# RMS normalisation with relu, 16384 rows of 512 floats: an unrolled program rewritten as hardware loops, with the arithmetic of a row regrouped

## The chip, the cores and the metric

One core of one Trainium2 chip. The metric is the device time of one execution in microseconds (us). The kernel before takes 164.29 us (median of 4 runs, 164.16 to 164.57). The profile is one traced execution, and its "span" (162.0 us) leaves out some 2 us of start and end that the time includes.

## The reference

```python
# x: 16 x 1024 x 512 float32; gamma: 512 ones; eps: 1e-5
rms = np.sqrt(np.mean(x ** 2, axis=-1, keepdims=True) + eps)
return np.maximum(x / rms * gamma, 0).astype(np.float32)
```

33.55 MB come in and 33.55 MB go out, and little arithmetic is done on them.

## The kernel before

The rows are cut into 8 chunks of 4 MB (128 partitions x 16 rows x 512). There are six slots in on-chip memory, so six loads can go out before any store, and a seventh waits until the first store has landed. All loads and stores are issued from SP, on one queue. A chunk is worked on in two groups of 8 rows.

```python
K = 16; G = 8; nslots = 6
junk = psum.tile([P, d], F32, name="junk")
...
def compute(i):
    xt = slot[i % nslots]
    for g in range(ngroups):                       # 2 groups of 8 rows
        a, b = g * G, (g + 1) * G
        for j in range(a, b):                      # ScalarE: sum of squares of a row
            nc.scalar.activation(out=junk, in_=xt[:, j, :], func=ACTF.Square,
                                 accum_out=ss[i][:, j:j + 1])
        nc.scalar.activation(out=rms[i][:, a:b], in_=ss[i][:, a:b],
                             func=ACTF.Sqrt, bias=eps_sb, scale=inv_d)
        nc.vector.tensor_mul(out=xt[:, a:b, :], in0=xt[:, a:b, :], in1=gammaG())
        nc.vector.reciprocal(out=rstd[i][:, a:b], in_=rms[i][:, a:b])
        for j in range(a, b):                      # VectorE: scale and relu of a row
            nc.vector.tensor_scalar(out=xt[:, j, :], in0=xt[:, j, :],
                scalar1=rstd[i][:, j:j + 1], scalar2=0.0, op0=ALU.mult, op1=ALU.max)
...
for i in range(min(nslots, nchunks)): load(i)
for i in range(min(nslots, nchunks)): compute(i)
nxt = nslots
for i in range(nchunks):
    store(i)
    if i >= 1 and nxt < nchunks:
        load(nxt); compute(nxt); nxt += 1
```

Everything is unrolled, and the framework places the semaphore waits. A wait that it places is carried by the waiting instruction itself.

Of the kernel before, what the change touches and what calls it, by code (L numbers as in the profile page):

```python
# [1 line left out]

# [4 lines left out]

F32 = mybir.dt.float32
ALU = mybir.AluOpType
ACTF = mybir.ActivationFunctionType  # L10


@with_exitstack
def kernel(
    ctx: ExitStack,
    tc: tile.TileContext,
    x: bass.AP,
    gamma: bass.AP,
    eps: bass.AP,
    out: bass.AP,  # L20
):


    nc = tc.nc
    P = nc.NUM_PARTITIONS

    x2 = x.flatten_outer_dims()
    out2 = out.flatten_outer_dims()
    n, d = x2.shape
    rows = n // P  # L30
    inv_d = 1.0 / d
    xv = x2.rearrange("(c p k) d -> c p k d", p=P, k=16)
    ov = out2.rearrange("(c p k) d -> c p k d", p=P, k=16)

    K = 16
    G = 8
    nchunks = rows // K
    nslots = 6
    ngroups = K // G

    singles = ctx.enter_context(tc.tile_pool(name="singles", bufs=1))
    slots = ctx.enter_context(tc.tile_pool(name="slots", bufs=1))
    small = ctx.enter_context(tc.tile_pool(name="small", bufs=1))
    psum = ctx.enter_context(
        tc.tile_pool(name="psum", bufs=1, space=bass.MemoryType.PSUM))

    ctx.enter_context(tc.manual_schedule())

    gseed = singles.tile([P, d], F32, name="gseed")
    gamma_sb = singles.tile([P, d], F32, name="gamma_sb")  # L50
    eps_sb = singles.tile([P, 1], F32, name="eps_sb")
    junk = psum.tile([P, d], F32, name="junk")
    slot = [slots.tile([P, K, d], F32, name=f"slot{s}") for s in range(nslots)]
    ss = [small.tile([P, K], F32, name=f"ss{i}") for i in range(nchunks)]
    rms = [small.tile([P, K], F32, name=f"rms{i}") for i in range(nchunks)]
    rstd = [small.tile([P, K], F32, name=f"rstd{i}") for i in range(nchunks)]

    def load(i):
        nc.sync.dma_start(out=slot[i % nslots], in_=xv[i])

    def store(i):
        nc.sync.dma_start(out=ov[i], in_=slot[i % nslots])

    def gammaG():
        g = gamma_sb[:]
        return bass.AP(tensor=g.tensor, offset=g.offset,
                       ap=[g.ap[0], [0, G], g.ap[1]])

    def compute(i):
        xt = slot[i % nslots]  # L70
        for g in range(ngroups):
            a, b = g * G, (g + 1) * G
            for j in range(a, b):
                nc.scalar.activation(out=junk, in_=xt[:, j, :], func=ACTF.Square,  # L74
                                     accum_out=ss[i][:, j:j + 1])
            nc.scalar.activation(out=rms[i][:, a:b], in_=ss[i][:, a:b],  # L76
                                 func=ACTF.Sqrt, bias=eps_sb, scale=inv_d)
            nc.vector.tensor_mul(out=xt[:, a:b, :], in0=xt[:, a:b, :], in1=gammaG())  # L78
            nc.vector.reciprocal(out=rstd[i][:, a:b], in_=rms[i][:, a:b])  # L79
            for j in range(a, b):  # L80
                nc.vector.tensor_scalar(  # L81
                    out=xt[:, j, :], in0=xt[:, j, :],
                    scalar1=rstd[i][:, j:j + 1], scalar2=0.0,
                    op0=ALU.mult, op1=ALU.max)

    nc.vector.memset(gseed, 0.0)  # L86
    nc.vector.memset(eps_sb, eps)  # L87
    for q in range(0, P, 32):
        nc.scalar.dma_start(out=gseed[q:q + 1, :], in_=gamma[None, :])

    for i in range(min(nslots, nchunks)):
        load(i)
    nc.vector.stream_shuffle(gamma_sb, gseed, [0] * 32)  # L93
    for i in range(min(nslots, nchunks)):
        compute(i)
    nxt = nslots
    for i in range(nchunks):
        store(i)
        if i >= 1 and nxt < nchunks:
            load(nxt)  # L100
            compute(nxt)
            nxt += 1


# [1 line left out]
_INS = ['x', 'gamma', 'eps']  # L106
_OUTS = [((16, 1024, 512), 'float32')]

_NUMBERS = {'eps': 9.999999747378752e-06}


# [26 lines left out]
```

## Time and profile before

| | before |
|---|---|
| time, median (lowest to highest) | 164.29 us (164.16 to 164.57) |
| span of the profile | 162.0 us |
| share of the 16 DMA engines' time on the data queue | 96.9% |
| VectorE (DVE) at work, first multiply to last row | 19.1 to 143.0 us |
| last store, issue to landing | 143.0 to 161.0 us |

The page of the kernel before. After the busy times come rows over 40 equal slices of the span: for DMA the mean busy share in tenths, then GB/s. The queue lines give packets, MB and share of the engines' time. In the group lines the numbers after the bar are busy us and mean ns of one, then idle time before them and what ended it.

```profile
span 162.0 us, 554 instructions
...
DVE 124.6 (77%) x164; ACT 98.5 (61%) x274; POOL 0.2 (0%) x4
...
DMA  6999899999999999998999999999999999999990
GB/s 227 421 405 502 388 413 493 390 421 477 396 421 471 396 388 388 461 445 388 463 437 404 453 445 404 453 437 396 461 429 445 429 421 445 429 421 445 437 413 16
...
q1 hardware_dynamic: 2304, 67.11, 96.9%
q14 instruction: 3, 0.02, 0.0%
...
DVE 74%; DMA 8%; ACT 3%; issue 2%; DVEq 0%
...
L74 ACT ACTIVATE junk<-slot 128x512 f32<-128x512 f32 x128 | 76.8, 600 | 23.0 <-DMA slot<-in_x_dram 19.5
L78 DVE TENSOR_TENSOR slot<-slot,gamma_sb 128x4096 f32<-128x4096 f32 x16 | 70.7, 4418 | 4.2 <-ACT junk L74 4.2
L81 DVE TENSOR_SCALAR slot<-slot,rstd 128x512 f32<-128x512 f32 x128 | 52.1, 481 | 0.6
```

The DMA row is full from end to end. The chain (the line that begins "DVE 74%") names VectorE all the same: VectorE is seamless too, and a chain can follow only one of two things that run side by side.

The timeline of the kernel before: start, duration, engine, operation, and in brackets the idle time before it. First lines: ScalarE's (ACT) first rows. Then a group on VectorE, and the end.

```profile
13.06 0.60 ACT L74 ACTIVATE junk<-slot 128x512 f32<-128x512 f32 x1 [8.57 <-DMA slot<-in_x_dram]
13.60 0.19 ACT L74 ACTIVATION_READ_ACCUMULATOR junk<-slot 128x1 f32 x1
13.81 0.60 ACT L74 ACTIVATE junk<-slot 128x512 f32<-128x512 f32 x1
...
19.09 4.42 DVE L78 TENSOR_TENSOR slot<-slot,gamma_sb 128x4096 f32<-128x4096 f32 x1 [4.16 <-ACT junk L74]
23.43 0.20 DVE L79 RECIPROCAL rstd<-rms 128x8 f32<-128x8 f32 x1
23.66 3.26 DVE L81 TENSOR_SCALAR slot<-slot,rstd 128x512 f32<-128x512 f32 x8
26.83 4.42 DVE L78 TENSOR_TENSOR slot<-slot,gamma_sb 128x4096 f32<-128x4096 f32 x1
...
139.73 3.26 DVE L81 TENSOR_SCALAR slot<-slot,rstd 128x512 f32<-128x512 f32 x8
143.01 0.33 SPq L62 DMA_DIRECT2D out_dram<-slot  x1
```

VectorE's group has a period of 7.74 us (26.83 - 19.09).

The waits of the SP queue before: who waited for what, total us, times, longest.

```profile
SPq L133 <- DMA out_dram<-slot: 17.6, 1, 17.6
```

The last store needs 17.6 us after its issue is done.

### The profile page before, as it was taken

How to read it: one execution, taken by the hardware profiler on the slowest of the kernel's cores; microseconds unless marked ns; L12 is line 12 of the kernel's file. 1: busy time of each engine (PE TensorE's matmuls, PEld its weight loads, DVE VectorE, ACT ScalarE, POOL GpSimd, SP SyncE). 2: the span in 40 equal slices, each digit the busy share in tenths (PEclk: the TensorE clock that was granted, in tenths of full speed). 3: DMA queues.
4: the chain of work that ended last, by engine and by line, in shares of the span. 5: the costliest groups of instructions: out<-in, count | busy, mean ns of one | idle time of the engine just before them, and what ended most of it. 6: DMA issues, size and time to landing. Idle time of an engine off the chain costs nothing.

```text
span 162.0 us, 554 instructions
## 1 busy us (share of the span) xinstructions
DVE 124.6 (77%) x164; ACT 98.5 (61%) x274; POOL 0.2 (0%) x4
## 2 busy tenths in 40 slices
DVE  1001299999999999999999999999999999920000
ACT  2107999999999999999999199901998000000000
POOL 0000000000000000000000000000000000000000
DMA  6999899999999999998999999999999999999990
GB/s 227 421 405 502 388 413 493 390 421 477 396 421 471 396 388 388 461 445 388 463 437 404 453 445 404 453 437 396 461 429 445 429 421 445 429 421 445 437 413 16
DMA packets 2315, 67.14 MB, mean 414 GB/s; under 512 B 260, under 2 KB 260, under 8 KB 264
## 3 DMA queue, kind: packets, MB, share of 16 engines
q1 hardware_dynamic: 2304, 67.11, 96.9%
q14 instruction: 3, 0.02, 0.0%
q10 hardware_dynamic: 8, 0.01, 0.0%
HBM read 33.56 MB, written 33.55 MB: 414 GB/s over the span
## 4 chain that ended last, share of the span: by engine, by line
DVE 74%; DMA 8%; ACT 3%; issue 2%; DVEq 0%
DVE slot L78 43%; DVE slot L81 30%; DMA slot<-in_x_dram 8%; ACT junk L74 3%; DVE rstd L79 1%; DVEq L133 0%
## 5 line engine op out<-in xcount | busy, mean ns | idle before, releaser
L74 ACT ACTIVATE junk<-slot 128x512 f32<-128x512 f32 x128 | 76.8, 600 | 23.0 <-DMA slot<-in_x_dram 19.5
L78 DVE TENSOR_TENSOR slot<-slot,gamma_sb 128x4096 f32<-128x4096 f32 x16 | 70.7, 4418 | 4.2 <-ACT junk L74 4.2
L81 DVE TENSOR_SCALAR slot<-slot,rstd 128x512 f32<-128x512 f32 x128 | 52.1, 481 | 0.6
L74 ACT ACTIVATION_READ_ACCUMULATOR junk<-slot 128x1 f32 x128 | 23.8, 186 | 0.0
L93 DVE LOAD_MASK_SELECT gamma_sb<-gseed x1 | 0.0, 14 | 12.8 <-DMA gseed<-in_gamma_dram 12.8
L76 ACT ACTIVATE rms<-ss,eps_sb 128x8 f32<-128x8 f32 x16 | 4.8, 301 | 0.5
L74 ACT ACT_TABLE_LOAD x1 | 1.3, 1283 | 3.2 <-issue 3.2
L79 DVE RECIPROCAL rstd<-rms 128x8 f32<-128x8 f32 x16 | 3.1, 194 | 0.0
L76 ACT ACT_TABLE_LOAD x1 | 1.3, 1283 | 0.0
L86 DVE MEMSET gseed<- 128x512 f32 x1 | 0.5, 485 | 0.9 <-PEq L119 0.9
L93 DVE STREAM_SHUFFLE gamma_sb<-gseed 128x512 f32<-128x512 f32 x1 | 0.7, 721 | 0.0
L119 POOL MEMSET const-bfloat16-1.0<- 128x1 bf16 x1 | 0.1, 101 | 0.0
L119 POOL MEMSET const-uint8-127<- 128x1 uint8 x1 | 0.1, 101 | 0.0
L119 POOL MEMSET const-float32-0.0<- 128x1 f32 x1 | 0.1, 99 | 0.2 <-issue 0.2
L119 POOL MEMSET const-float32-1.0<- 128x1 f32 x1 | 0.1, 98 | 0.0
L87 DVE MEMSET eps_sb<- 128x1 f32 x1 | 0.1, 59 | 0.0
## 6 DMA issues: line engine op xcount, KB each, us to landing
slot<-in_x_dram SPq DMA_DIRECT2D x8, 4096.0 KB, 30.6
out_dram<-slot SPq DMA_DIRECT2D x8, 4096.0 KB, 35.4
gseed<-in_gamma_dram ACTq DMA_DIRECT2D x4, 2.0 KB
```

Of the source, the lines that this page charges most:

```text
L74: nc.scalar.activation(out=junk, in_=xt[:, j, :], func=ACTF.Square, accum_out=ss[i][:, j:j + 1])
L76: nc.scalar.activation(out=rms[i][:, a:b], in_=ss[i][:, a:b], func=ACTF.Sqrt, bias=eps_sb, scale=inv_d)
L78: nc.vector.tensor_mul(out=xt[:, a:b, :], in0=xt[:, a:b, :], in1=gammaG())
L79: nc.vector.reciprocal(out=rstd[i][:, a:b], in_=rms[i][:, a:b])
L81: nc.vector.tensor_scalar(out=xt[:, j, :], in0=xt[:, j, :], scalar1=rstd[i][:, j:j + 1], scalar2=0.0, op0=ALU.mult, op1=ALU.max)
L86: nc.vector.memset(gseed, 0.0)
L87: nc.vector.memset(eps_sb, eps)
L93: nc.vector.stream_shuffle(gamma_sb, gseed, [0] * 32)
L119: nc = _bacc.Bacc("TRN2", target_bir_lowering=False, num_devices=1)
```

## The change

Its intent: a shorter program and cheaper waits. The loops over groups become hardware loops on ScalarE and VectorE with semaphores of the kernel's own; one activation table is loaded ahead instead of two; the gamma multiply over 8 rows and the scale-and-relu per row become (x*rstd)*gamma per row and one relu over 8 rows.

```diff
+    junk = psum.tile([P, G, d], F32, name="junk")          # a scratch row for each of the 8
-        nc.sync.dma_start(out=slot[i % nslots], in_=xv[i])
+        nc.sync.dma_start(out=slot_ap(i), in_=xv[i]).then_inc(sem_ld[i], 16)
...
+        for i in range(nchunks):                            # GpSimd relays the landings
+            nc.gpsimd.wait_ge(sem_ld[i], 16)
+            nc.gpsimd.sem_inc(ready, per)
...
+        nc.scalar.preload_act_table(ACTF.Sqrt)
+        with nc.scalar.Fori(0, ngroups) as gi:
+            nc.scalar.wait_ge(ready, 1)
+            nc.scalar.sem_inc(ready, -1)
+            ...                                             # 8 squares, the last one: then_inc(sa, 1)
+            nc.scalar.wait_ge(sa, 1)
+            nc.scalar.sem_inc(sa, -1)
+            ...                                             # root: then_inc(sq, 1)
-            nc.vector.tensor_mul(out=xt[:, a:b, :], in0=xt[:, a:b, :], in1=gammaG())
-            nc.vector.reciprocal(out=rstd[i][:, a:b], in_=rms[i][:, a:b])
-            for j in range(a, b):
-                nc.vector.tensor_scalar(... op0=ALU.mult, op1=ALU.max)
+        with nc.vector.Fori(0, ngroups) as gi:
+            nc.vector.wait_ge(sq, 1)
+            nc.vector.sem_inc(sq, -1)
+            nc.vector.reciprocal(out=rstd[:, bass.ds(col, G)],
+                                 in_=rms[:, bass.ds(col, G)]).then_inc(sv, 1)
+            nc.vector.wait_ge(sv, 1)
+            nc.vector.sem_inc(sv, -1)
+            for j in range(G):
+                row = slots[:, bass.ds(base + j * d, d)]
+                r = nc.vector.scalar_tensor_tensor(
+                    out=row, in0=row, scalar=rstd[:, bass.ds(col + j, 1)], in1=gamma_sb,
+                    op0=ALU.mult, op1=ALU.mult)             # the last one: then_inc(sv, 1)
+            nc.vector.wait_ge(sv, 1)
+            nc.vector.sem_inc(sv, -1)
+            nc.vector.tensor_scalar_max(out=blk, in0=blk, scalar1=0.0).then_inc(done, 1)
```

The order of loads and stores on SP stays as it was.

## The prediction

> **What bounds the kernel now.** The transfers. Over the span of 162.0 us the SP queue's packets fill 96.9% of the 16 DMA engines' time (queue table); by stretches the DMA share is 0.97 to 1.05 from 5 to 155 us, at 420 to 453 GB/s. The Trainium skill ("DMA: Bandwidth & Descriptors", Bandwidth) gives 435 GB/s as the fabric's ceiling; the trace agrees. The chain of waits names VectorE (74%), because its work from 19.1 to 143.0 us is seamless and the last store follows it. But that store takes 17.6 us to land (waits of the SP queue), where the first load, at the head of the queue, needs 12.3 us. So the last store queues some 5.3 us behind others: VectorE has that much slack.
>
> **What changes, per group of 8 rows.** VectorE before, start to start (the chain): gamma multiply 4.33, reciprocal 0.12, eight row operations 0.41 apart (3.26): 7.74 us, 16 groups 123.9. After, the row operation reads two tensors. The Trainium skill ("VectorE: DVE Perf Modes", the perf-mode tier table) has fp32 one-source operations at double rate, two-tensor ones at single rate; the trace agrees: 4418 ns for 4096 elements against 481 for 512. Estimates from these: a row is 512 x 1.042 = 533 ns plus the 214 that the present row has over 267, so 747 ns long, 0.67 apart, eight rows 5.46; relu over 4096 elements at double rate 2.2; reciprocal 0.19. Together 7.85. Two waits on VectorE's own semaphore become instructions of their own, the first followed by a register instruction, where today reciprocal to row leaves 0.03 us. I guess 0.3 and 0.2 us for them; no record of before shows such a sequence. Sum 8.35 us, 0.6 more per group. Branch and address arithmetic should hide under the relu and the rows.
>
> **Head.** One table load (1.28 us) goes, but it lay beside VectorE's first multiply and gains nothing. VectorE now starts after the first root instead of beside it, and the landing is relayed through GpSimd: start about 20.1 instead of 19.1. ScalarE (0.76 us per row, about 6.9 per group) stays faster than VectorE, off the path.
>
> **Sum.** VectorE ends at 20.1 + 16 x 8.35 = 153.7 instead of 143.0, 10.7 later; slack absorbs 5.3; the end moves by some 5 us, less if the guessed waits are smaller (8.15 per group: about 2). The transfers are the same bytes in the same order. I predict 168.3 us, 80% range 165.0 to 172.5. Chances: faster by over 2% 0.01, within 2% 0.41, slower by over 2% 0.58.
>
> **What the profile would show.** Right: rows near 745 ns, 0.67 apart; relu near 2.28 us; VectorE's group period 8.15 to 8.6, its end at 150 to 157 us; the DMA share falling for 2 to 8 us before the last store; that store landing in about 12 us. Wrong: a period of 8.0 or less (the slack swallows all, the time stays near 164), or a last store that still queues.
>
> **What would make it wrong.** Own-semaphore waits nearly free; a row operation with less fixed cost than the present one; or, to the other side, a branch or register instructions that stall VectorE by a microsecond per group (+16 us), or ScalarE's loop becoming the slower one. The store alone may land in other than 12.3 us, which moves the end by as much.

## The result, and the profile after

| | before | after |
|---|---|---|
| time, median (lowest to highest), 4 runs each | 164.29 us (164.16 to 164.57) | 165.41 us (165.27 to 165.50) |
| ratio | | 1.0065 (95%: 1.0048 to 1.0083) |
| span | 162.0 us | 163.5 us |
| VectorE's first operation; period of a group; end | 19.09; 7.74; 142.99 us | 19.29; 8.24; 151.25 us |
| last landing, from the span's start | 160.97 us | 162.38 us |
| from VectorE's end to the last landing | 17.98 us | 11.13 us |

A ratio is the mean time of one kernel's fast runs over that of the other's of the same rounds, so it is not quite the ratio of the medians quoted. The change costs 0.65%: within 2%, but clear of noise.

The page after:

```profile
span 163.5 us, 1007 instructions
...
DVE 126.0 (77%) x164; ACT 86.3 (53%) x273; POOL 0.2 (0%) x4
...
DMA  6999999899999999989999999999999999993985
GB/s 232 409 394 498 393 433 465 385 473 425 401 489 393 425 345 417 481 385 441 457 401 473 409 409 441 433 433 433 417 433 457 417 433 433 441 433 160 385 385 257
...
q1 hardware_dynamic: 2304, 67.11, 96.3%
...
L108 ACT ACTIVATE junk<-slots 128x512 f32 x128 | 74.5, 582 | 30.5 <-ACTq L104 30.2
L132 DVE SCALAR_TENSOR_TENSOR slots<-slots,rstd,gamma_sb 128x512 f32 x128 | 86.2, 747 | 4.8 <-DVEq L129 4.8
L139 DVE TENSOR_SCALAR slots<-slots x16 | 36.7, 2294 | 2.4 <-DVEq L138 0.2
```

The DMA row now has a hole (the 3, slice 37, 147 to 151 us, 160 GB/s): the engines had run out of work when VectorE delivered the last chunk. The q14 line is gone. A row costs 747 ns, the relu 2294.

The timeline after, the same places:

```profile
13.55 0.60 ACT L108 ACTIVATE junk<-slots 128x512 f32 x1 [8.97 <-ACTq L104]
14.08 0.19 ACT L108 ACTIVATION_READ_ACCUMULATOR junk<-slots  x1
14.18 0.58 ACT L108 ACTIVATE junk<-slots 128x512 f32 x1
...
19.29 0.20 DVE L126 RECIPROCAL rstd<-rms  x1 [4.27 <-DVEq L122]
19.79 5.39 DVE L132 SCALAR_TENSOR_TENSOR slots<-slots,rstd,gamma_sb 128x512 f32 x8 [0.30 <-DVEq L129]
25.34 2.29 DVE L139 TENSOR_SCALAR slots<-slots  x1 [0.16 <-DVEq L138]
27.54 0.20 DVE L126 RECIPROCAL rstd<-rms  x1
...
148.96 2.29 DVE L139 TENSOR_SCALAR slots<-slots  x1
151.28 0.33 SPq L74 DMA_DIRECT2D out_dram<-slots  x1
```

Here are the two waits that became instructions of their own: 0.30 us after the reciprocal, about 0.16 us before the relu. And ScalarE's second row (14.18) begins 0.09 us before the accumulator of the first has been read (14.27): over a group rows come about 0.61 us apart instead of 0.76, because each has a scratch row of its own. The Trainium skill ("ScalarE: Activation LUTs", What ACT_TABLE_LOAD costs) says that back-to-back activations overlap by about 93 ns. After agrees (0.09 us, counted to the accumulator read that ends the row ahead); before had spent that on its wait: each row carries a wait for the accumulator read of the row ahead.

The waits of the SP queue after. The line counts from where the queue comes to wait, about 1 us later than the issue, from which the store takes 11.10 us; the 11.13 us above count from VectorE's end.

```profile
SPq L144 <- DMA out_dram<-slots: 10.1, 1, 10.1
```

### The profile page after: what moved, and what is told of

Its sections match the earlier page's. It is cut to its first block, busy times and chain, and to the rows that moved or that the text cites. A ratio compares the mean times of both kernels' runs of the same rounds, so it can differ in the third digit from the quotient of the medians.

```text
span 163.5 us, 1007 instructions
## 1 busy us (share of the span) xinstructions
DVE 126.0 (77%) x164; ACT 86.3 (53%) x273; POOL 0.2 (0%) x4
## 5 line engine op out<-in xcount | busy, mean ns | idle before, releaser
L108 ACT ACTIVATE junk<-slots 128x512 f32 x128 | 74.5, 582 | 30.5 <-ACTq L104 30.2
L132 DVE SCALAR_TENSOR_TENSOR slots<-slots,rstd,gamma_sb 128x512 f32 x128 | 86.2, 747 | 4.8 <-DVEq L129 4.8
L139 DVE TENSOR_SCALAR slots<-slots x16 | 36.7, 2294 | 2.4 <-DVEq L138 0.2
L108 ACT ACTIVATION_READ_ACCUMULATOR junk<-slots x128 | 23.9, 187 | 0.0
L126 DVE RECIPROCAL rstd<-rms x16 | 3.2, 197 | 4.3 <-DVEq L122 4.3
L115 ACT ACTIVATE rms<-ss,eps_sb x16 | 4.8, 301 | 3.0 <-ACTq L114 3.0
```

What stands on the lines that cost most here:

```text
L108: a = nc.scalar.activation(out=junk[:, j, :], in_=slots[:, bass.ds(base + j * d, d)], func=ACTF.Square, accum_out=ss[:, bass.ds(col + j, 1)])
L115: nc.scalar.activation(out=rms[:, bass.ds(col, G)], in_=ss[:, bass.ds(col, G)], func=ACTF.Sqrt, bias=eps_sb, scale=inv_d).then_inc(sq, 1)
L126: nc.vector.reciprocal(out=rstd[:, bass.ds(col, G)], in_=rms[:, bass.ds(col, G)]).then_inc(sv, 1)
L132: r = nc.vector.scalar_tensor_tensor(out=row, in0=row, scalar=rstd[:, bass.ds(col + j, 1)], in1=gamma_sb, op0=ALU.mult, op1=ALU.mult)
L139: nc.vector.tensor_scalar_max(out=blk, in0=blk, scalar1=0.0).then_inc(done, 1)
```

## The experiments

A "ring" here is the list of packets of one of the 16 DMA engines; each transfer is spread over all 16. **Theory A**: the last landing is the later of two times: a floor, at which 16 busy rings have moved all the bytes, and VectorE's end plus the 11.1 us of a store alone. The kernel before lies on the floor with slack to spare, the one after on the second branch. **Rival B**: VectorE's end sets the time in both. **Rival C**: the half microsecond per group is the new arithmetic, not the waits. **Rival D**: the loops and semaphores cost the 1.1 us by themselves, whatever VectorE does. During the work a further idea came up, theory F, about program text.

Before was run again beside each experiment, on the same chip; over the four chips used its median was 163.97, 164.49, 164.21 and 164.81 us, so each kernel is compared with before of its own rounds. Last landings are from the traces.

### Eight scratch tiles in the kernel before (e2_before_eight_banks)

```diff
-    junk = psum.tile([P, d], F32, name="junk")
+    junk = [psum.tile([P, d], F32, name=f"junk{j}") for j in range(G)]
...
-                nc.scalar.activation(out=junk, in_=xt[:, j, :], ...
+                nc.scalar.activation(out=junk[j % G], in_=xt[:, j, :], ...
```

> The kernel before, with eight one-bank scratch tiles instead of one, so that a row of ScalarE no longer waits for the row ahead of it. Theory A (the transfers set the end, VectorE has slack): ScalarE's rows come 0.61 us apart instead of 0.76, VectorE starts at about 18.0 us instead of 19.1 and ends about 1.1 us earlier, the last store lands no earlier (about 161.0 us) and takes about 18.7 us instead of 17.6, time 164.3, same within 0.3 us. Rival B (the chain of waits is right, VectorE's end sets the time): 1.1 us faster, about 163.2.

Measured: 163.90 us against 163.97 for before in the same rounds, ratio 0.9998 (0.9970 to 1.0027). The timeline:

```profile
13.50 0.19 ACT L74 ACTIVATION_READ_ACCUMULATOR junk<-slot 128x1 f32 x1
13.59 0.58 ACT L74 ACTIVATE junk<-slot 128x512 f32<-128x512 f32 x1
...
18.00 4.42 DVE L78 TENSOR_TENSOR slot<-slot,gamma_sb 128x4096 f32<-128x4096 f32 x1 [3.06 <-ACT junk L74]
```

VectorE starts 1.09 us earlier and stores the last chunk at 141.97 instead of 143.01 us, and the last landing stays at 160.97 us. That is A to the hundredth, and B is out. It also shows what made ScalarE's rows faster in the changed kernel: the scratch tiles, not the loop. (The mirror image, the changed kernel with one scratch tile, was not run.)

### Each half of the change alone (e3_loops_old_sums, e4_before_new_sums)

The loops and semaphores of after, with the arithmetic of before:

```diff
...                                                            # ahead of the loop: a wait for gamma's shuffle
             nc.vector.reciprocal(...).then_inc(sv, 1)
+            blk3 = blk.rearrange("p (k d) -> p k d", d=d)
+            nc.vector.tensor_mul(out=blk3, in0=blk3, in1=gammaG()).then_inc(sv, 1)
-            nc.vector.wait_ge(sv, 1)
-            nc.vector.sem_inc(sv, -1)
+            nc.vector.wait_ge(sv, 2)
+            nc.vector.sem_inc(sv, -2)
             for j in range(G):
-                r = nc.vector.scalar_tensor_tensor(...)      # and the second wait and the relu go
+                r = nc.vector.tensor_scalar(out=row, in0=row, scalar1=rstd[:, bass.ds(col + j, 1)],
+                    scalar2=0.0, op0=ALU.mult, op1=ALU.max)  # the last one: then_inc(done, 1)
```

> The changed kernel's loops and semaphores with the arithmetic of before (gamma multiply over 8 rows, then scale and max per row). Theory A: the loss per group lies in the waits that became instructions of their own. Only one such wait is left per group, so the period is about 7.74 + 0.35 = 8.1 us, VectorE ends near 149, under the limit of about 149.8 from which the end moves; time 164.3 to 164.8. Rival C (the arithmetic costs the half us per group, the waits nothing): period 7.75, VectorE's end near 143.

The unrolled kernel of before, with the arithmetic of after:

```diff
-            nc.vector.tensor_mul(out=xt[:, a:b, :], in0=xt[:, a:b, :], in1=gammaG())
             nc.vector.reciprocal(out=rstd[i][:, a:b], in_=rms[i][:, a:b])
             for j in range(a, b):
-                nc.vector.tensor_scalar(... op0=ALU.mult, op1=ALU.max)
+                nc.vector.scalar_tensor_tensor(out=xt[:, j, :], in0=xt[:, j, :],
+                    scalar=rstd[i][:, j:j + 1], in1=gamma_sb, op0=ALU.mult, op1=ALU.mult)
+            nc.vector.tensor_scalar_max(out=xt[:, a:b, :], in0=xt[:, a:b, :], scalar1=0.0)
```

> The kernel before, unrolled and with its own scheduling of waits, with the arithmetic of after (two-tensor row operation, one relu per 8 rows). Theory A: waits carried by the instructions themselves cost 0.03 us, so the period is 0.23 + 5.39 + 0.05 + 2.2 = 7.87 us, VectorE starts near 20.7 (the second table load is now ahead of it), ends near 146.7, inside the slack; time 164.3. Rival C: period 8.2, end near 152, time 165.5 or more.

Measured: the loops with the old sums take **163.01 us against 163.97**, ratio 0.9944 (0.9915 to 0.9972), faster than both kernels. The unrolled one with the new sums takes 163.82, ratio 0.9983 (0.9957 to 1.0010), the same as before.

The timeline of the loops with the old sums:

```profile
27.51 0.20 DVE L133 RECIPROCAL rstd<-rms  x1
27.62 4.38 DVE L136 TENSOR_TENSOR slots<-slots,gamma_sb 128x4096 f32 x1
32.15 3.26 DVE L141 TENSOR_SCALAR slots<-slots,rstd  x8 [0.16 <-DVEq L138]
35.32 0.20 DVE L133 RECIPROCAL rstd<-rms  x1
...
144.87 0.33 SPq L79 DMA_DIRECT2D out_dram<-slots  x1
```

The timeline of the unrolled kernel with the new sums:

```profile
28.52 0.19 DVE L78 RECIPROCAL rstd<-rms 128x8 f32<-128x8 f32 x1
28.75 5.39 DVE L80 SCALAR_TENSOR_TENSOR slot<-slot,rstd,gamma_sb 128x512 f32<-128x512 f32 x8
34.17 2.29 DVE L84 TENSOR_SCALAR slot<-slot 128x4096 f32<-128x4096 f32 x1
36.38 0.20 DVE L78 RECIPROCAL rstd<-rms 128x8 f32<-128x8 f32 x1
```

The periods split the half microsecond. The new arithmetic with carried waits: 36.38 - 28.52 = 7.86 us, 0.12 more than before. After, the same operations take 8.24: the waits as instructions of their own, with the address computation behind the first, are the other 0.38. Rival C is out: the arithmetic is a quarter of it. In the loops with the old sums the reciprocal's wait hides behind the 4.4 us multiply, and the period is 7.81; I had expected 8.1.

What no theory expected: the loops with the old sums store their last chunk 1.86 us later than before does (144.87 against 143.01) and yet end about 1.0 us earlier, with the last landing at 159.94 instead of 160.97 us. The floor itself is lower in the looped program.

### The transfers alone (e9_transfers_alone; the result is wrong)

The body of before without its arithmetic and without the load of gamma: the loads and stores of the rows, in their order.

> Wrong result on purpose: the loads and stores of before in their order, no arithmetic. Theory A: the same transfers take the same time, last landing at 160.5 to 161.2 us, time 164.0 to 164.4. Rival B: without VectorE's 124 us the time falls clearly below 163.

Measured: 162.05 us, ratio to before 0.9882 (0.9849 to 0.9916), last landing at 159.12 us. Its page:

```profile
span 159.9 us, 61 instructions
...
q1 hardware_dynamic: 2304, 67.11, 98.1%
```

A's figure missed, and B's, a time clearly below 163, was met. B is out all the same: with VectorE's 124 us gone, the time falls by only 1.9. But those 1.9 us are not transfers, against A as I had put it.

The increments of the last store's semaphore tell where those go. Each of the 16 rings adds one when its share has landed, and the store counts as landed with the slowest. Worked out from the semaphore records of the traces, which no view prints, us from the span's start (the q14 packets are the 8 KB ones that the trace shows on the instruction queue between the first data and the last landing):

```
                                   q14    8th of 16 up   14th    15th    last    last - 8th
transfers alone                     0      158.57       158.76  158.78  159.12      0.55
loops with the old sums             0      158.97       159.12  159.55  159.94      0.97
before                              3      158.85       159.28  159.42  160.97      2.12
unrolled with the new sums          3      158.74       159.38  159.79  161.22      2.48
before, one more op per group       4      159.25       159.55  160.74  162.46      3.21
```

The middle ring ends at the same time in all, within 0.7 us. What differs is one ring, or two, that come late, and by more than 1.0 us only in the programs that fetch program text while they run. In before the latest ring's last 32 KB packet starts after its neighbours have finished, and takes 1.21 us. The earlier landings of before tell the same in part: the last increment lags the middle one by 0.3 to 0.5 us ahead of the second of its three fetches (at 31.5, 50.9 and 79.8 us), by 0.8 to 1.1 after it and by 1.4 to 1.6 after the third. The last step, to 2.1 at the landing at 112.6 us, has no fetch beside it. The programs without a fetch drift in that stretch too: the loops with the old sums from 0.3 us at the landing at 101.4 us to 1.0 at the end. So fetches are not the whole of the lag, and why rings drift apart without one is open. If the drift is the same in both programs, fetches account for the 1.15 us by which before's lag exceeds that of the loops. What has fallen behind is not caught up by the end.

**Theory F**: each 8 KB fetch of program text sets one of the 16 rings back by about a microsecond, and where the rings are always full this is paid at the end. **Rival G**: the unrolled program's extra microsecond comes from its waits or its order of issue.

### Using up the slack (e5_before_one_more, e6_before_two_more)

Before, with one or two more VectorE operations after each group, whose result nobody reads:

```diff
+    spare = singles.tile([P, 2, d], F32, name="spare")
...
+            for t in range(1):      # range(2) in the second kernel
+                nc.vector.tensor_scalar_max(out=spare[:, t, :], in0=gamma_sb, scalar1=0.0)
```

> The kernel before with one more VectorE operation of about 0.33 us after each group (15 of them lie ahead of the last store). Theory A (last landing = the later of 161.0 us and VectorE's end + 11.1 us, so 6.5 us of slack): VectorE ends near 148.0, inside the slack; time 164.3, unchanged within 0.3. Rival B (VectorE's end sets the time): +5 us. The slack of the prediction (5.3 us) says unchanged too.

> The same with two more operations per group: VectorE ends near 153. Theory A: 3.3 us past the slack of 6.5, last landing near 164, time near 167.4 (+3.1). With the prediction's slack of 5.3 us: +4.6, near 168.9. Rival B: +10.

Measured: one more, 165.09 us against 164.49, ratio 1.0034 (1.0014 to 1.0054). Two more, 167.12 us, ratio 1.0158 (1.0137 to 1.0178). The waits of the SP queue with two more:

```profile
SPq L136 <- DMA out_dram<-slot: 10.7, 1, 10.7
```

With two more the last store is issued at 153.27 us and lands 11.08 us later, at 164.35. A holds: past the slack, the end is VectorE's end plus a store alone. The loss of 2.6 us was 0.5 less than expected. The miss is the run with one more: A said unchanged, and VectorE was inside the slack (the store issued at 148.23, so 159.3 from that branch), but the last landing moved to 162.46. The table above has it: the longer program fetches a fourth time, at 142.0 us, and two rings come late. The lag goes from 2.5 us at the landing at 132.7 us to 3.6 at the one at 143.4. The floor moved, as F says.

### VectorE well inside the slack (e7_after_no_relu; the result is wrong)

```diff
                 if j == G - 1:
-                    r.then_inc(sv, 1)
-            nc.vector.wait_ge(sv, 1)
-            nc.vector.sem_inc(sv, -1)
-            nc.vector.tensor_scalar_max(out=blk, in0=blk, scalar1=0.0).then_inc(done, 1)
+                    r.then_inc(done, 1)
```

> Wrong result on purpose: the changed kernel without its relu (2.2 us of VectorE per group and one wait). Theory A: VectorE's period falls to about 6.05 us, its end to about 116 to 120 us, and the time only to the transfers' floor, about 164.3 (-1.1 against after), the last store queueing again for 17 us or more. Rival D (the loops, semaphores and tail of the changed kernel cost the 1.1 us, not VectorE): still 165.4.

Measured: 162.86 us against 164.49 for before, ratio 0.9910 (0.9889 to 0.9931). The timeline:

```profile
129.09 0.33 SPq L74 DMA_DIRECT2D out_dram<-slots  x1
```

The last store is issued at 129.09 us and the last landing is at 159.97. (VectorE was expected to end by 120 us and ended at 129: it had to wait 8.5 and 8.0 us before the last two chunks.) The last store goes out 15.8 us earlier than in the loops with the old sums and lands no sooner: the time stops falling at a floor, as A says. And D is out: the changed kernel's loops, its relay, its first wait and its tail cost nothing against before. The floor is that of the loops with the old sums (159.94), 1 us under before's, where I had still expected 164.3.

### One load alone (e8_first_load_alone)

```diff
             load(i)
+            if i == 0:
+                nc.sync.wait_ge(sem_ld[0], 16)
```

> The changed kernel, with the second load held back until the first has landed. Asked: why the first load needs 12.2 us and the last store, alone, 11.1. If the loads queued behind it slow the first load: it lands 11.1 us or less after its issue here. If a load alone is simply slower than a store alone: still 12.2. The queue then runs dry for about 2 us, so the transfers' floor is some 2 us later: time 165.4 to 166.5.

Measured: 165.66 us, ratio to before 1.0069 (1.0046 to 1.0093). The first load lands 12.4 us after its issue at 0.94, no sooner than with five loads queued behind it (12.2 in after); the second, on empty rings again, needs about 12.1. So a 4 MB load alone takes about 12.2 us and a 4 MB store alone about 11.1, and the first is no stand-in for the second. Why, this run does not tell.

### Program text added (e10_loops_pool_program, e11_transfers_512, e12_transfers_1024, e13_loops_semaphores_late)

Three kernels give GpSimd, which has little to do, a long program:

```diff
 # transfers alone, 512 or 1024:
+    for t in range(512):
+        nc.gpsimd.memset(spare[:, t:t + 1], 0.0)
 # loops with the old sums, after each relay:
             nc.gpsimd.sem_inc(ready, per)
+            for t in range(64):
+                nc.gpsimd.memset(spare[:, 64 * i + t:64 * i + t + 1], 0.0)
```

> Wrong result on purpose: the transfers alone (162.05 us) with 512 one-column memsets on GpSimd. Theory F: about 4 fetches, the last increment lags by 2 to 5 us instead of 0.5, time 163.3 to 167. Rival G: 162.0.

> The same with 1024 memsets. Theory F: twice the fetches (about 8), and twice the added lag and time of the run with 512 if they share a ring, about the same if they spread over rings. Rival G: 162.0.

> The third experiment's kernel (loops, sums of before, 163.0 us) with 64 one-column memsets on GpSimd after each chunk's relay, 512 in all, whose result nobody reads. Theory F (each 8 KB fetch of program text takes a turn of about 1.2 us on one of the 16 rings, and a load or store lands with its slowest ring): about 4 fetches appear on the instruction queue, the last increment of the last store lags the median one by 2 to 5 us instead of 1.0, time 164 to 167. Rival G (the unrolled kernel's extra 1 us comes from its waits or its order of issue, and fetches cost nothing): no change, 163.0.

Measured: the transfers alone take 162.05 us without the memsets, 164.97 with 512 (ratio to before 1.0044, 1.0024 to 1.0063) and 167.59 with 1024 (1.0216, 1.0192 to 1.0240), on another chip than the run without; against before of their own rounds the ratio climbs from 0.988 by 1.6 and 3.3 points. The lines of the instruction queue and of the memsets with 1024:

```profile
q14 instruction: 8, 0.07, 0.1%
...
L88 POOL MEMSET spare<- 128x1 f32 x1024 | 34.2, 98 | 9.5 <-issue 9.2
```

With 512 there are 4 packets. By the same records of the last store:

```
                                   q14    8th of 16 up   14th    15th    last    last - 8th
transfers alone                     0      158.57       158.76  158.78  159.12      0.55
with 512 memsets                    4      158.66       158.90  159.03  162.47      3.81
with 1024 memsets                   8      158.74       159.00  159.03  164.11      5.37
```

Fifteen rings keep their time; one falls behind, by 3.3 us more with four fetches and 4.8 us more with eight. Part of the four's came late: read at the first landing after the last fetch (24.9 and 47.0 us), the lag is 2.34 and 4.95 us over that of the transfers alone, 0.6 us per fetch in both and twice as much for twice the fetches, as F says for one ring. The rest of the four's grew after 54 us, with no fetch. A packet of 8 KB itself is recorded with 0.31 us, so a fetch costs its ring more than its own duration; why is open. The memsets run in the same stretch as the fetches, so these two runs alone do not tell them apart; the last run below has none.

The third kernel settles nothing by itself. It took 164.77 us (ratio 1.0048, 1.0029 to 1.0066), but its memsets slowed VectorE: eight rows took 4.08 and 5.15 us in its first groups instead of 3.26, the last store was issued at 150.11 instead of 144.87, and most rings' last increments came at 161.1, 11 us later. It had moved to the other branch. So I ran it once more with program text that touches no memory:

```diff
             nc.gpsimd.sem_inc(ready, per)
+            if i == 5:
+                for t in range(256):
+                    nc.gpsimd.sem_inc(spin, 1)      # a semaphore nobody waits for
+                    nc.gpsimd.sem_inc(spin, -1)
```

> The third experiment's kernel again (163.0 us), with 512 increments and decrements of a semaphore that nobody waits for on GpSimd after the sixth chunk's relay: program text to be fetched, and no access to the on-chip memory that could slow VectorE, as the memsets of the tenth experiment did (its row operations stretched from 3.26 to 5.15 us and VectorE ended 5 us later, so it settles nothing by itself). Theory F, at the 0.7 us per fetch of the runs with the transfers alone: 4 fetches, VectorE's end unchanged near 144.9, the last increment lags the median by 3 to 4.5 us instead of 1.0, time 165 to 166.3. Rival G: 163.0, lag 1.0.

Measured: 164.84 us against 164.81 for before, ratio 1.0016 (0.9994 to 1.0039), where the same kernel without this text had 0.9944. The end of the timeline and the queue line:

```profile
144.90 0.33 SPq L80 DMA_DIRECT2D out_dram<-slots  x1
```

```profile
q14 instruction: 5, 0.03, 0.0%
```

VectorE ends where it did. Four of the five packets are of 8 KB (at 71 to 101 us). The 8th ring is up at 158.92 us, the last three come at 160.32, 161.48 and 161.71, a lag of 2.8 us instead of 1.0. The gain of the loops is gone, by program text alone. That fetches cost nothing, as rival G had it, is out. That before's own extra microsecond is its three fetches is not shown as directly: before without them was not run. The size is under what I had expected (165 to 166.3): the setbacks fell on three rings instead of one, and the latest counts.

## Why the prediction was right or wrong

It said 168.3 us, 4.0 over before; measured was 165.41, 1.1 over. The direction and the mechanism were right, and the range (165.0 to 172.5) holds the result, but the stated size is over three and a half times the measured one (and the headline was already under the text's own sum of 5.4), and "slower by over 2%" had the larger chance.

**Right.** The transfers bound the kernel; VectorE's seamless work did not (eight scratch tiles, 1.04 us earlier, nothing gained). Rows were put at 747 ns and measured 747, eight of them 5.46 us against 5.39, and the relu at 2.2 to 2.28 us against 2.29. The Trainium skill ("VectorE: DVE Perf Modes", the perf-mode tier table) gave the rates, and the trace agrees. The new waits would cost more than the loop's branch, and the DMA row would empty before the last store: both seen.

**The step that failed is "Sum"**: "VectorE ends at 20.1 + 16 x 8.35 = 153.7 instead of 143.0, 10.7 later; slack absorbs 5.3". Three terms were mis-sized, all to the same side:

| term | predicted | measured | effect on the end |
|---|---|---|---|
| VectorE's start | 20.1 us | 19.29 us | -0.8 us |
| period of a group, x16 | 8.35 us | 8.24 us | -1.7 us |
| last store, alone | 12.3 us | 11.1 us | -1.2 us |

- The start: ScalarE's rows were carried over at 0.76 us each. The diff gives each of the 8 rows its own scratch row, which takes away a wait per row, and eight rows come 1.2 us sooner. I had read this part of the diff as bookkeeping.
- The period: the operations without the new waits were right (7.85 us, measured 7.86 in the unrolled kernel with the new sums). The waits, guessed at 0.5 us, cost 0.38. Small per group, but there are sixteen.
- The slack: the first load was taken as the stand-in for a store alone. Loads alone need 12.1 to 12.4 us, the store 11.1.

Between VectorE's end and the last landing the prediction allowed 17.6 us before, of which 12.3 would stay. Measured from VectorE's end, it was 17.98, of which 11.13 stayed: 6.85 us of slack, not 5.3. VectorE ended 8.26 us later, not 10.7; 8.26 - 6.85 = 1.41 us is what the last landing moved. The time moved 1.12.

**Not seen at all**: the change also does good. It leaves no fetch of program text on the DMA rings, and the floor is about 159.95 us instead of 160.97. After cannot show it, because it ends on the other branch. With the arithmetic of before, whose one wait hides behind a long multiply, the same loops show it: 163.01 us against 163.97. So part of before's slack was itself the wait for a ring that a fetch had set back.

**Open**: why a fetch costs its ring twice its recorded 0.31 us; which rings get the fetches of which engine; why rings drift apart without a fetch, and with it the 0.8 us by which the loops with no fetch (159.94) still end after the transfers alone (159.12); and why a store alone is faster than a load alone.

## What to carry to other kernels

When transfers fill the span, write the end as the later of two sums, the rings' floor and the last producer's end plus one transfer alone, and get the slack between them from a transfer of the same direction before you price an engine's loss. Multiply by the number of groups only what you have measured: 0.1 us of guess in a loop of sixteen was the largest single error here. And look at the instruction queue where all rings are full, because a large transfer lands with its slowest ring: a fetch of program text counts there, and a loop that removes it is worth something even where its branches and waits are not free.

## What the Trainium skill lacked or had wrong

- "Runtime: NRT & Kernel Launch", Instruction fetch mechanics, calls the cost of crossing a block of program text "mostly hidden" and has kernels prefer full unrolling. From VectorE it is hidden here (its period is 7.74 us all through before's three fetches); from GpSimd with memsets back to back it is not (9.2 us idle in seven stops with 1024 of them), nor on rings that are always full: 0.6 us per fetch on one ring (162.05 us without fetches, 164.97 with four, 167.59 with eight). The loops with the same arithmetic beat the unrolled program by 0.6%. The page gives the block as 16 KiB or 256 instructions; here 1024 added instructions brought 8 packets of 8 KB, one at a time, 5.5 us apart.
- "VectorE: DVE Perf Modes", The DRAIN you can't avoid, has a semaphore after each operation cost nothing extra. True here for a wait carried by the instruction (0.03 us from reciprocal to row). A wait on the engine's own semaphore that stands as an instruction of its own, followed by an address computation, left 0.30 us, and about 0.16 us without one. No page read for this has that difference.
- "DMA: Bandwidth & Descriptors" gives no times of a load and a store of one size side by side for this chip. For 4 MB on empty rings the runs show 12.1 to 12.4 us for a load and 11.1 for a store.
- "SBUF — State Buffer" has the port pair that VectorE and GpSimd share as an exclusive lock, which one side waits for. The tenth experiment agrees in kind (eight 0.48 us rows took up to 5.30 us instead of 3.26 beside GpSimd's one-column memsets; in two groups the rows kept their 3.26 us and the 64 memsets took 3.14 and 2.82 instead of 2.17); what such small operations cost VectorE no page says.
